# Loading x and the adaLN weights for two blocks of features at a time at the head of a one-core encoder layer

## The chip, the cores and the metric

The kernel runs on one core of one Trainium2 chip. The metric is the device time of one execution in microseconds (us): 1555.84 is the median of three runs (1552.31 to 1558.68). A second number is the profile: one execution recorded by the hardware profiler, whose own time was 1556.39 and whose span, from the first to the last recorded instruction, was 1554.6. Matrix products run on TensorE (PE; its weight loads are PEld), elementwise work on VectorE (DVE), ScalarE (ACT) and GpSimd (POOL); transfers are issued in order by a queue of SyncE (SP) or of POOL and carried out by 16 DMA engines.

## The reference

One layer of a streaming encoder, for a prompt of 1024 tokens and a sample of 32 tokens, width 1024. What matters here is its first step:

```
m = silu(c) @ w_ada + b_ada             # c: one vector per sequence; w_ada: 1024 x 6144
sh1, sc1, g1, sh2, sc2, g2 = split(m, 6)
u = x * (1 + sc1) + sh1                 # 1024 x 1024
z = u @ w_in                            # fq | fk | fv | ff | dq | dk | dv
... forgetting attention, differential attention, output projection,
... layer norm, ConvFFN, layer norm
```

The shift `sh1` and the scale `sc1` of a feature need the whole column of `w_ada` of that feature, and the product `u @ w_in` sums over features, so the kernel can begin the product for a block of features as soon as that block's columns of `w_ada` and its part of `x` are there.

## The kernel before

Features are cut into eight blocks of 128 (k = 0 to 7), tokens into eight blocks of 128. In the first stage, which the change is about, each block k of features goes through these steps:

- **Loads.** `ada_mod` loads 1 MB of `w_ada`: 128 columns for the shift and 128 for the scale, in four transfers of 256 KB (line 175) into tiles of tag `ada` (four buffers, two per block, so two blocks fit). `modulated` loads 512 KB of `x`, 128 features for all tokens (line 317), into a tile of tag `x` (two buffers). For every even k, 512 KB of `w_in` for two blocks come in (`wrfq`, line 320; the "raw" weights).
- **Columns.** 8 products of `silu(c)` with the `w_ada` tiles, column-tiled on PE into the PSUM tile `psAm` (`colmm`; the trace counts two records for each, so 16 for a block). ACT copies them to `asb` (line 181), small products with a selector matrix sum up the groups ("selector products": `psAm<-cst,asb`), and DVE adds the bias and writes `sh`, `sc` (lines 186 and 187).
- **Transposes.** 8 transposes of `x` into two PSUM banks `psx` (line 116), one of tag `pt`, one of tag `ms`. Since `psf` holds the other `pt` bank, the transposes of the next block can write a bank only when ACT and DVE have read it.
- **Modulation.** For each of two halves of 512 tokens, ACT writes the rounded `uh` (line 330), DVE `uf` in full (line 331) and the rest `ul = uf - uh` (line 332).
- **Products.** `products_fq`: for four groups of 128 columns, three matmuls (high with high, low with high, high with low) into `accqa`, `accqb`, for the first 512 tokens only. The raw weights are split into a high and a low part by ACT (line 88) and DVE (line 89) first. For every odd k four products into `psf` (forget gates) follow, which read the `uf` tiles of both blocks.

The order on PE, SP and DVE in this stage is the order of the code (`manual_schedule`); on ACT, on POOL and in the rest of the kernel a scheduler puts the instructions in order from its own estimate of times, so an edit here may also move instructions elsewhere. Semaphores hold each instruction until its inputs are there and its buffer is free. After the stage come, on PE, the one small transpose `psp`, the products of the other 512 tokens (`accqc`, `accqd`), and the five other column groups of `w_in` (`z1` to `z5`).

Around `k`, the body before reads: sums of block k+1, transposes of block k+1, half of the products of block k, modulation of block k+1, columns of block k+2, the other half of the products of block k. Loads are issued two blocks ahead.

Of the kernel before, what the change touches and what calls it, by code (L numbers as in the profile page):

```python
# [8 lines left out]
F32 = mybir.dt.float32  # L9
# [7 lines left out]
P = 128  # L17
# [36 lines left out]
def layer_kernel(ctx: ExitStack, tc: tile.TileContext, a: dict, o: list):  # L54
# [59 lines left out]
    def tr(out, in_):  # L114
        n = in_.shape[0]
        nc.tensor.transpose(out, in_, ident[:n, :n])  # L116
# [52 lines left out]
    def ada_mod(pl, name, kb, j0, sh, sc, tag):  # L169
# [17 lines left out]
        nc.vector.tensor_scalar(sc[:, kb], ps[:, 258:260], b[1], 1.0, ALU.add, ALU.add)  # L187
        yield

    def gate(pl, i, j0, h, tag):  # L190
# [76 lines left out]
    with pool("pa") as pa:  # L267
        def pt_(name, tag, bufs, shape=(P, 1024), dt=F32):
            return pa.tile(list(shape), dt, name=name, tag=tag, bufs=bufs)


        xk0, uf0 = pt_("x0", "x", 2, (P, TT)), pt_("uf0", "x2", 2, (P, TT))
# [38 lines left out]
        nc.gpsimd.dma_start(wff, w_in[:, :, 1536:1544])  # L311
        us_ = {}

        def modulated(k):

            xk = (pt_(f"x{k}", "x", 2, (P, TT)) if k else xk0)[:, 0:T].rearrange("p (b c) -> p b c", b=NB)
            nc.sync.dma_start(xk, xv[:, :, k * P:(k + 1) * P])
            if k % 2 == 0:
                raw = pt_(f"wrfq{k}", "raw", 5, (P, 2, 512)) if k else raw0
                nc.sync.dma_start(raw, w_in[:, k:k + 2, 0:512])  # L320
                raws.append(raw)
            yield
            psx = [b1(f"psx{k}{h}", "ms" if h else "pt") for h in range(2)]
            for i in range(8):
                tr(psx[i // 4][:, i % 4 * P:(i % 4 + 1) * P], xk[:, i])
            yield
            us_[k] = u = (pt_(f"uf{k}", "x2", 2, (P, TT)) if k else uf0)[:, 0:T]
            for h in range(2):
                t = slice(h * 512, (h + 1) * 512)
                nc.scalar.activation(uh[k][:, t], psx[h], AF.Identity, bias=sh1[:, k, 0:1], scale=sc1[:, k, 0:1])  # L330
                nc.vector.tensor_scalar(u[:, t], psx[h], sc1[:, k, 0:1], sh1[:, k, 0:1], ALU.mult, ALU.add)
                nc.vector.tensor_tensor(ul[k][:, t], u[:, t], f(uh[k][:, t]), ALU.subtract)
            yield

        def split_fq(k):
            if k < 5:
                hl = pq.tile([P, 2, 512], F32R, name=f"whfq{k}", tag="qk0", bufs=6)
            else:
                hl = pt_(f"whfq{k}", "hl", 5, (P, 2, 512), F32R) if k > 5 else hl5
            split(hl[:, 0], hl[:, 1], raws[k // 2][:, k % 2])  # L340
            hls.append(hl)

        def products_fq(k, prs, h):
            t = slice(h * 512, (h + 1) * 512)
            for pr in prs:
                c = slice(pr * P, (pr + 1) * P)
                mm3(acc[pr], hls[k][:, 0, c], hls[k][:, 1, c], uh[k][:, t], ul[k][:, t], k == 0, k == KD - 1)

        with tc.manual_schedule(engines={e.engine for e in (nc.tensor, nc.sync, nc.vector)}):
            am = [ada_mod(pa, f"m{k}", k, 0, sh1, sc1, "po") for k in range(KD)]  # L350
            xm = [modulated(k) for k in range(KD)]
            for k in range(2):
                next(am[k])
                next(xm[k])
            next(am[0])
            next(xm[0])
            next(am[0])
            split_fq(0)
            next(xm[0])
            next(am[1])  # L360
            for k in range(KD):
                if k + 2 < KD:
                    next(am[k + 2])
                    next(xm[k + 2])
                elif k + 2 == KD:
                    nc.sync.dma_start(xs[0:TS], a["x_sample"][0])
                    nc.sync.dma_start(rot, a["cst"][:, C_RES:C_END])
                if k + 1 < KD:
                    next(am[k + 1])
                    next(xm[k + 1])  # L370
                    split_fq(k + 1)
                products_fq(k, (0, 1), 0)
                if k % 2 == 1:
                    for j in range(4):
                        kk, h = k - 1 + j % 2, j // 2
                        mm(psf[32 * j:32 * j + 8], wff[:, kk], us_[kk][:, h * 512:(h + 1) * 512], k == 1, k == KD - 1, tile_position=(0, 32 * j))
                if k + 1 < KD:
                    next(xm[k + 1])
                if k + 2 < KD:
                    next(am[k + 2])  # L380
                products_fq(k, (2, 3), 0)
        ps = b1("psp", "ms")
        tr(ps[:, 48:r0 + 17], prow[0:NJ + 17])
        nc.vector.tensor_copy(pcol[:, 48:r0 + 17], ps[:, 48:r0 + 17])
# [18 lines left out]
        ffr = pt_("ffr", "x", 2)[0:8]  # L403
# [62 lines left out]
        def forget():  # L466
            psl = b1("psl", "ms")
            for b in range(NB):
                tr(psl[:, b * 8:(b + 1) * 8], ffr[:, b * P:(b + 1) * P])
            for k in range(KD):  # L470
                colmm(psl[:, 64:72], us[:, k], wff[:, k], k, KD)
            lfp, lfs, lfc = [lg[:, 512 + 64 * i:576 + 64 * i].rearrange("p (b h) -> p b h", h=8) for i in range(3)]
            ffs = lg[0:TS, 704:712]
            sum_groups(ffs, psl[:, 64:72], TS)
            lfs = lfs[0:TS, 0:1]
            nc.sync.dma_start(lfc, a["cache_fox_logf"][0, 0].rearrange("(p j) h -> p j h", j=8))
            log_sigmoid(lfp, psl[:, 0:64].rearrange("p (b h) -> p b h", h=8), P, NB)
# [42 lines left out]

        def ld_a(nm):
            ldn.append(0)
            return pt_(nm, "x" if len(ldn) % 2 else "x2", 2)
# [991 lines left out]
```

## Time and profile before

| | us |
|---|---|
| median of three runs | 1555.84 |
| profiled execution, own time | 1556.39 |
| its span | 1554.6 |
| PE busy | 1482.9 (95%) |
| DVE, ACT, POOL busy | 875.0, 582.1, 422.1 |
| mean granted TensorE clock, share of full | 0.983 |

PE is busy for 95% of the span, so the 71.7 us in which it is not are all that a new order of the same work can win, with what a lower clock costs. The page cuts the span into 40 slices of 38.9 us; in its first slice PE shows a 6, in later ones mostly a 9, and the DMA engines a 9 (this slice is the first stage). Waits of DVE, ACT and POOL cost nothing as long as PE has work.

### The profile page before, as it was taken

What the parts mean: (1) busy time and instruction counts of PE and PEld (TensorE: products, weight loads), DVE (VectorE), ACT (ScalarE), POOL (GpSimd) and SP (SyncE); (2) the same over time, 40 slices, a digit from 0 to 9 for tenths busy, and PEclk for the clock granted to TensorE, in tenths of its full rate; (3) what the DMA queues carried; (4) which work ended last, traced back from release to release, by engine and by line L of the source; (5) the groups of instructions that cost most, each with busy time, mean ns of one, the idle gap of its engine ahead of it and who ended that gap; (6) DMA issues with size and microseconds to landing.
All of it is one profiled execution on the core that took longest, in us unless ns stands there. A gap on an engine that the chain in (4) does not pass through costs nothing.

```text
span 1554.6 us, 23531 instructions
## 1 busy us (share of the span) xinstructions
PE 1482.9 (95%) x8525; PEld 1242.0 (80%) x8525; DVE 875.0 (56%) x1772; ACT 582.1 (37%) x1187; POOL 422.1 (27%) x638
## 2 busy tenths in 40 slices
PE   6999999997989999989999999999999999999996
PEld 4677787765646677777789999999999998888884
DVE  3522217734535799847768886742233236446788
ACT  3311211245646788743654344321121121322332
POOL 0002005734323333323414433455530000000001
PEclk9999999998999999999999999999999999999998
DMA  9623123459775344244448999832231113555863
GB/s 255 190 97 114 55 86 112 122 175 259 189 210 138 96 125 98 85 164 145 150 162 307 337 358 322 295 116 74 80 92 55 41 41 114 183 176 179 288 224 135
DMA packets 221141, 250.52 MB, mean 161 GB/s; under 512 B 14465, under 2 KB 148898, under 8 KB 221026
## 3 DMA queue, kind: packets, MB, share of 16 engines
q1 hardware_dynamic: 210962, 218.65, 45.0%
q0 software_dynamic: 10064, 30.37, 6.6%
q8 instruction: 67, 1.10, 0.3%
q14 instruction: 48, 0.39, 0.1%
HBM read 173.83 MB, written 66.75 MB: 155 GB/s over the span
## 4 chain that ended last, share of the span: by engine, by line
PE 65%; DMA 15%; DVE 9%; issue 4%; SPq 2%; ACT 2%; POOL 2%; POOLq 0%; DVEq 0%; ACTq 0%
PE wd L82 15%; PE up L82 8%; PE upc L82 4%; DMA dwn<-wn 4%; PE wo L82 4%; PE po L82 3%; DMA dres<-rr 3%; DMA rr<-dx 2%; PE Sf L82 2%; PE ptf L116 2%; PE Sd L82 2%; DVE wn L89 2%; PE pod L82 1%; DMA wq<-in_w_down 1%; SPq L175 1%
## 5 line engine op out<-in xcount | busy, mean ns | idle before, releaser
L82 PE MATMUL wd<-ol,oh 128*128 128x512 f32 x308 | 119.4, 390 | 0.0
L82 PE MATMUL wd<-oh,ol 128*128 128x512 f32 x308 | 117.1, 389 | 0.0
L82 PE MATMUL wd<-oh 128*128 128x512 f32 x308 | 112.9, 391 | 2.3 <-DMA oh<-dwn 2.3
L982 POOL TENSOR_TENSOR rstd<-rstd,mhalf 128x1 f32<-128x1 f32 (+1 forms) x18 | 14.5, 814 | 262.3 <-DVE rstd L981 257.6
L1162 POOL TENSOR_TENSOR rr<-rr,gb 128x128 f32<-128x128 f32 (+1 forms) x72 | 45.8, 637 | 117.6 <-DMA rr<-dx 117.2
L629 POOL TENSOR_SCALAR wf<-wf,rs 128x128 f32<-128x128 f32 (+7 forms) x64 | 47.6, 749 | 109.5 <-DVE rs L595 80.1
L82 PEld LDWEIGHTS wd<-oh 128*128 128x128 f32 x308 | 57.6, 188 | 16.6 <-DMA oh<-dwn 2.0
L82 PEld LDWEIGHTS wd<-ol,oh 128*128 128x128 f32 x308 | 57.8, 188 | 12.5 <-DMA ol<-dwn 0.6
L82 PEld LDWEIGHTS wd<-oh,ol 128*128 128x128 f32 x308 | 57.8, 188 | 12.0
L88 ACT CAST oh<-h 128x512 fp32r<-128x512 f32 x44 | 27.2, 621 | 87.3 <-PE wd L82 67.7
L89 DVE TENSOR_TENSOR wh<-wr,wh 128x512 fp32r<-128x512 f32 x40 | 28.7, 742 | 50.9 <-ACT wh L88 50.9
L88 ACT CAST wh<-wr 128x512 fp32r<-128x512 f32 x40 | 24.3, 622 | 85.4 <-DMA wr<-in_w_in 19.0
L594 ACT ACTIVATE wf<-wf,lo 128x128 f32<-128x128 f32 (+7 forms) x64 | 49.5, 776 | 17.8 <-DVE lo L591 15.6
L594 ACT ACTIVATE wd<-wd,lo 128x128 f32<-128x128 f32 (+7 forms) x64 | 49.6, 777 | 13.3 <-DVE lo L591 11.3
L82 PE MATMUL po<-ptpf,vf 128*64 128x256 f32 (+1 forms) x320 | 54.0, 372 | 0.5 <-DVE ptpf L619 0.4
L1205 ACT ACTIVATE cv<-cv 128x1058 f32<-128x1058 f32 x22 | 24.0, 1090 | 76.5 <-DVE cv L1204 76.4
L591 DVE CUSTOM_DVE_ANT_0 wf<-Sf,nb 128x512 f32<-128x512 f32 (+3 forms) x64 | 36.8, 588 | 26.4 <-PE Sf L82 19.1
L1163 POOL TENSOR_TENSOR rr<-rr,gb 128x128 f32<-128x128 f32 (+1 forms) x72 | 50.2, 698 | 5.2
L1200 POOL COPY cvo<-row 128x2 f32<-128x2 f32 x22 | 12.8, 584 | 138.9 <-ACT row L1198 138.9
L89 DVE TENSOR_TENSOR ol<-h,oh 128x512 fp32r<-128x512 f32 x44 | 29.8, 683 | 36.4 <-ACT oh L88 36.4
L1197 ACT COPY row<-up 128x352 f32<-128x352 f32 x44 | 17.7, 455 | 83.4 <-PE up L82 56.8
L116 PE MATMUL ptf<-cst,wf 128*128 128x128 f32 x288 | 47.6, 286 | 1.1 <-POOL wf L629 0.7
(1545 smaller groups left out, 4777.5 us busy)
## 6 DMA issues: line engine op xcount, KB each, us to landing
dwn<-wn SPq DMA_DIRECT2D x154, 256.0 KB
oh<-dwn SPq DMA_DIRECT2D x77, 256.0 KB
ol<-dwn SPq DMA_DIRECT2D x77, 256.0 KB
wq<-in_w_down SPq DMA_DIRECT2D x44, 256.0 KB
wr<-in_w_in SPq DMA_DIRECT2D x20, 512.0 KB
adam<-in_w_ada SPq DMA_DIRECT2D x32, 256.0 KB
adan<-in_w_ada SPq DMA_DIRECT2D x32, 256.0 KB
ga<-in_w_ada SPq DMA_DIRECT2D x16, 512.0 KB
```

Source lines behind the costliest of these rows:

```text
L82: nc.tensor.matmul(out, l, r, start=start, stop=stop, **k)
L88: nc.scalar.copy(hi, src)
L89: (eng or nc.vector).tensor_tensor(lo, src, f(hi), ALU.subtract)
L116: nc.tensor.transpose(out, in_, ident[:n, :n])
L175: nc.sync.dma_start(pga[h][:, :, s, :], w_ada[:, 4 * h:4 * h + 4, c0:c0 + P])
L591: nc.vector.tensor_tensor_reduce(w[:, c], S[:, 0:n], t, -1.0, lo, ALU.add, ALU.min, lo_)
L594: nc.scalar.activation(w[:, 0:ext], w[:, 0:ext], AF.Exp, bias=lo, scale=-1.0, accum_out=sm)
L629: nc.gpsimd.tensor_scalar(w, w, rs, 1.0, ALU.mult, ALU.mult)
L1162: nc.gpsimd.tensor_tensor(r, r, gb[c0][0:n, 0], ALU.mult)
L1163: nc.gpsimd.tensor_tensor(r, r, gb[c0][0:n, 1], ALU.add)
L1197: nc.scalar.copy(row[:, 2 + g * G3:2 + (g + 1) * G3], accs[g])
L1205: nc.scalar.activation(c[:, 0:L], c[:, 0:L], AF.Silu)
```

## The change

The loads of `x` and `w_ada` are made for two blocks at a time: `ada_pair` loads 2 MB in four transfers of 512 KB, with rows of 256 columns (1 KB) in place of 128 columns (512 B), and `load_x` loads 1 MB of `x` for two blocks, also in rows of 1 KB. The memory stays the same: the four `ada` buffers now hold one pair (before, two blocks), and `x` has one buffer of double size (before, two). The columns of a pair are computed in one go, and all 12 products of a block stand in one run.

```diff
+    def ada_pair(pl, name, p, j0, sh, sc, tag):
+        pga = {}
+        for s in range(2):
+            for h in range(2):
+                pga[h, s] = t = pl.tile([P, 4, 2 * P], F32, name=f"ada{name}{h}{s}", tag="ada", bufs=4)
+                c0 = (j0 + s) * D + 2 * p * P
+                nc.sync.dma_start(t, w_ada[:, 4 * h:4 * h + 4, c0:c0 + 2 * P])
+        yield
...
+                colmm(ps[:, s * 256:(s + 1) * 256], cT[:, k, :], pga[k // 4, s][:, k % 4], k, KD)
+            asb.append(ca.tile([P, 256], F32, name=f"asb{s}", tag="s256", bufs=4))
+            nc.scalar.copy(asb[s], ps[:, s * 256:(s + 1) * 256])
+        yield
...
+        def load_x(p):
+            t = xk0 if p == 0 else pt_(f"x{p}", "x", 1, (P, 2 * TT))
+            xp_[p] = t = t[:, 0:2 * T].rearrange("p (b c) -> p b c", b=NB)
+            nc.sync.dma_start(t, xv[:, :, 2 * p * P:2 * (p + 1) * P])
...
-            for k in range(2):
-                next(am[k])
-                next(xm[k])
             next(am[0])
+            load_x(0)
+            load_raw(0)
             next(xm[0])
+            next(am[0])
             next(am[0])
             split_fq(0)
             next(xm[0])
-            next(am[1])
             for k in range(KD):
...
+                p = k // 2
+                if k % 2 == 0 and p + 1 < KD // 2:
+                    next(am[p + 1])
+                    load_raw(p + 1)
                 if k + 1 < KD:
-                    next(am[k + 1])
                     next(xm[k + 1])
+                if k % 2 == 0:
+                    if p + 1 < KD // 2:
+                        load_x(p + 1)
...
+                products_fq(k, range(4), 0)
+                if k + 1 < KD:
                     split_fq(k + 1)
-                products_fq(k, (0, 1), 0)
-                if k % 2 == 1:
+                if k % 2 == 0:
+                    next(xm[k + 1])
+                    if p + 1 < KD // 2:
+                        next(am[p + 1])
+                else:
+                    if p + 1 < KD // 2:
+                        next(am[p + 1])
+                        next(xm[k + 1])
...
-                if k + 1 < KD:
-                    next(xm[k + 1])
-                if k + 2 < KD:
-                    next(am[k + 2])
-                products_fq(k, (2, 3), 0)
...
-                lft = pt_(f"lft{s}", "x", 2, (P, TT))[0:8]
+                lc = pt_(f"lc{s}", "x", 1, (P, 2 * TT))[0:8]
+                lft = lc[:, 0:TT]
...
-                cum = pt_(f"cum{s}", "x", 2, (P, TT))[0:8]
+                cum = lc[:, TT:2 * TT]
```

On SP, at the start of the program, the loads stand as follows before; `adam` are tiles of `w_ada`, `x` and `wrfq` those of `x` and of the raw weights:

```order
L175 DMA adam_153<-in_w_ada 128x4x128 x2
L175 DMA adam_154<-in_w_ada 128x4x128 x2
L317 DMA x_108<-in_x_prompt 128x8x128
L320 DMA wrfq_110<-in_w_in 128x2x512
L175 DMA adam_161<-in_w_ada 128x4x128 x2
L175 DMA adam_162<-in_w_ada 128x4x128 x2
L317 DMA x_167<-in_x_prompt 128x8x128
```

In the changed program the same place of SP reads, with the semaphores that each instruction waits for (`PE` stands for products that must have read the buffer, `DMAHW` for an earlier transfer):

```order
L197 DMA adam_159<-in_w_ada 128x4x256
L347 DMA x_108<-in_x_prompt 128x8x256 [waits DMAHW0_49]
L351 DMA wrfq_110<-in_w_in 128x2x512 [waits DMAHW1_49]
L485 DMA bfb<-in_b_f 128x8 [waits DMAHW2_49]
L545 DMA t_129<-in_conv_w 66x128 [waits DMAHW3_49,PE_49]
L546 DMA t_129<-in_state_ffn_conv 44x128 [waits DMAHW4_49]
L547 DMA t_129<-in_lambda_vecs 128x256 [waits DMAHW5_49]
L197 DMA adam_211<-in_w_ada 128x4x256 [waits DMAHW6_49,PE_49]
L197 DMA adam_213<-in_w_ada 128x4x256 [waits DMAHW7_49,PE_49]
L197 DMA adam_215<-in_w_ada 128x4x256 [waits DMAHW0_49,PE_49]
L197 DMA adam_217<-in_w_ada 128x4x256 [waits DMAHW1_49,PE_49]
L351 DMA wrfq_219<-in_w_in 128x2x512 [waits DMAHW2_49]
```

The `x` of the first blocks now stands behind 2 MB of `w_ada` in place of 1 MB, and the second pair of `w_ada` waits for products of the first.

On PE, between the products of block 1 and those of block 2, the program before reads (`psAm_313<-cst,asb` are the selector products of block 2, `psx_344`, `psx_345` the transposes of block 3):

```order
L82 MATMUL psAm_313<-adam_271,cT 32x256 x4
L82 MATMUL psAm_313<-adam_272,cT 32x256 x4
L82 MATMUL accqb<-uh_113,whfq_238 128x512
L82 MATMUL accqb<-ul_121,whfq_238 128x512
L82 MATMUL accqb<-uh_113,whfq_238 128x512 x2
L82 MATMUL accqb<-ul_121,whfq_238 128x512
L82 MATMUL accqb<-uh_113,whfq_238 128x512
L82 MATMUL psAm_313<-cst,asb 128x2 x2
L116 MATMUL psx_344<-cst,x_277 128x128 x4
L116 MATMUL psx_345<-cst,x_277 128x128 x4
L82 MATMUL accqa<-uh_114,whfq_293 128x512
```

Between the same products, the changed program reads (`asb_264`, `asb_274` belong to blocks 2 and 3, `psx_330`, `psx_331` are the transposes of block 3, `uh_114` is block 2):

```order
L82 MATMUL accqb<-uh_113,whfq_245 128x512
L82 MATMUL psAm_255<-cst,asb_264 128x2 x2
L82 MATMUL psAm_255<-cst,asb_274 128x2 x2
L82 MATMUL psf<-uf_109,wff 8x512
L82 MATMUL psf<-uf_248,wff 8x512
L82 MATMUL psf<-uf_109,wff 8x512
L82 MATMUL psf<-uf_248,wff 8x512
L116 MATMUL psx_330<-cst,x_231 128x128 x4
L116 MATMUL psx_331<-cst,x_231 128x128 x4
L82 MATMUL accqa<-uh_114,whfq_298 128x512
```

Before, the transposes of block 2 stood ahead of block 1's products, and half of those products stood behind the start of block 2's columns; now nothing but `psf` stands between the selector products of a pair and the transposes that need the banks of its modulation. In the attention stage, which the diff does not touch, the scheduler has put many pieces of PE's program in another order too.

## Rows read from the trace of the kernel before

**Rows 1.** Busy time by stretch: engine busy us, granted clock, DMA share, GB/s.
```profile
0.00:67.00 67.00, 50.85 (x333) 34.53 (x334) 32.72 (x70) 23.45 (x39) 3.78 (x10) 0.95 0.92 243
67.00:135.00 68.00, 68.00 (x316) 53.48 (x315) 14.41 (x24) 10.29 (x16) 4.37 (x6) 1.00 0.21 71
```
**Rows 2.** Stretches with 512 B rows alone, and with 2 and 4 KB rows.
```profile
40.00:44.00 4.00, 4.00 (x34) 3.08 (x27) 2.62 (x6) 2.34 (x5) 0.00 (x0) 1.00 1.19 291
100.00:103.00 3.00, 3.00 (x15) 2.48 (x14) 0.59 (x2) 0.75 (x2) 0.54 (x1) 1.00 1.02 387
```
**Rows 3.** Order of time on PE: start, us, engine, line, what, count [idle before].
```profile
12.37 1.97 PE L116 MATMUL psx<-cst,x 128*128 128x128 f32 x8 [0.60 <-DMA x<-in_x_prompt]
...
17.36 1.08 PE L82 MATMUL psAm<-adam,cT 128*32 128x256 f32 x8 [0.64 <-DMA adam<-in_w_ada]
...
21.39 0.78 PE L82 MATMUL accqa<-uh,whfq 128*128 128x512 f32 x1
...
28.93 0.61 PE L82 MATMUL psAm<-cst,asb 128*128 128x2 f32 x4 [2.67 <-ACT asb L181]
...
55.62 0.61 PE L82 MATMUL psAm<-cst,asb 128*128 128x2 f32 x4 [2.10 <-ACT asb L181]
```
**Rows 4.** The chain of work that ended last: start, us, what.
```profile
25.96 1.14 ACT whfq L88 x2
...
31.16 2.31 PE accqa L82 x6
33.47 0.97 PE psf L82 x8
...
37.24 0.93 PE psx L116 x8
38.17 1.39 PE accqa L82 x6
39.56 1.00 PE psAm L82 x16
...
42.16 0.36 PE psAm L82 x4
...
72.82 0.18 PE psp L116
```
**Rows 5.** The two stretches with a lower granted clock.
```profile
30.00:35.00 5.00, 5.00 (x36) 3.25 (x34) 1.02 (x2) 1.55 (x2) 0.00 (x0) 0.70 1.06 273
55.00:60.00 5.00, 4.38 (x22) 3.21 (x26) 2.56 (x6) 2.02 (x4) 0.00 (x0) 0.69 1.06 252
```
**Rows 6.** Order of time on DVE, one block's modulation.
```profile
37.47 0.21 DVE L186 TENSOR_SCALAR sh<-psAm,pcol 128x2 f32<-128x2 f32 x1
...
38.72 0.81 DVE L331 TENSOR_SCALAR uf<-psx,sc,sh 128x512 f32<-128x512 f32 x1 [0.31 <-ACT uh L330]
...
40.17 0.80 DVE L331 TENSOR_SCALAR uf<-psx,sc,sh 128x512 f32<-128x512 f32 x1
...
42.63 0.22 DVE L186 TENSOR_SCALAR sh<-psAm,pcol 128x2 f32<-128x2 f32 x1 [0.92 <-PE psAm L82]
```
**Rows 7.** Order of time on ACT: the same modulation; a cast waiting for its load; the scan's copy.
```profile
37.91 1.45 ACT L330 ACTIVATE uh<-psx,sh,sc 128x512 fp32r<-128x512 f32 x2 [2.16 <-DVE sc L187]
...
102.25 1.14 ACT L88 CAST wh<-wr 128x512 fp32r<-128x512 f32 x2 [2.62 <-DMA wr<-in_w_in]
...
166.70 1.19 ACT L492 COPY lft<-pslt 8x512 f32<-8x512 f32 x1 [4.89 <-PE pslt L116]
```
**Rows 8.** Order of time on SP: that load with three more; the scan's result.
```profile
96.88 2.50 SPq L534 DMA_DIRECT2D wr<-in_w_in  x4
...
164.15 0.30 SPq L503 DMA_DIRECT2D dcump<-cum  x1
```
**Rows 9.** PE's waits, 310 to 660 us: us in total, times, longest.
```profile
PE psAn L82 <- DMA adan<-in_w_ada: 7.3, 3, 4.6
PE psG L82 <- DMA ga<-in_w_ada: 3.6, 1, 3.6
```

More of the change, by code (lines that the diff above doesn't have):

```diff
@@ L188, in ada_mod @@
         yield
+    def ada_pair(pl, name, p, j0, sh, sc, tag):
[6 more added lines that the diff above has]
+        yield
+        ps = b1(f"psA{name}", tag)
+        asb = []
+        for s in range(2):
+            for k in range(KD):
+                colmm(ps[:, s * 256:(s + 1) * 256], cT[:, k, :], pga[k // 4, s][:, k % 4], k, KD)
+            asb.append(ca.tile([P, 256], F32, name=f"asb{s}", tag="s256", bufs=4))
+            nc.scalar.copy(asb[s], ps[:, s * 256:(s + 1) * 256])
+        yield
+        for s in range(2):
+            for q in range(2):
+                i = 4 * s + 2 * q
+                mm(ps[:, i:i + 2], asb[s][:, q * P:(q + 1) * P], cst[:, C_SEL2:C_SEL2 + 2], True, True)
+        for q in range(2):
+            kb = 2 * p + q
+            b = [bcol[:, (j0 + s) * 8 + kb:(j0 + s) * 8 + kb + 1] for s in range(2)]
+            nc.vector.tensor_scalar(sh[:, kb], ps[:, 2 * q:2 * q + 2], b[0], None, ALU.add)
+            nc.vector.tensor_scalar(sc[:, kb], ps[:, 4 + 2 * q:6 + 2 * q], b[1], 1.0, ALU.add, ALU.add)
+        yield
     def gate(pl, i, j0, h, tag):
@@ L269, in pt_ @@
             return pa.tile(list(shape), dt, name=name, tag=tag, bufs=bufs)
-        xk0, uf0 = pt_("x0", "x", 2, (P, TT)), pt_("uf0", "x2", 2, (P, TT))
+        xk0, uf0 = pt_("x0", "x", 1, (P, 2 * TT)), pt_("uf0", "x2", 2, (P, TT))
         raw0 = pt_("wrfq0", "raw", 5, (P, 2, 512))
@@ L312, in layer_kernel, with load_raw @@
         us_ = {}
-        def modulated(k):
[L316 to L322, printed above, removed]
+        xp_ = {}
+        def load_x(p):
+            t = xk0 if p == 0 else pt_(f"x{p}", "x", 1, (P, 2 * TT))
+            xp_[p] = t = t[:, 0:2 * T].rearrange("p (b c) -> p b c", b=NB)
+            nc.sync.dma_start(t, xv[:, :, 2 * p * P:2 * (p + 1) * P])
+        def load_raw(p):
+            raw = pt_(f"wrfq{p}", "raw", 5, (P, 2, 512)) if p else raw0
+            nc.sync.dma_start(raw, w_in[:, 2 * p:2 * p + 2, 0:512])
+            raws.append(raw)
+        def modulated(k):
             psx = [b1(f"psx{k}{h}", "ms" if h else "pt") for h in range(2)]
             for i in range(8):
-                tr(psx[i // 4][:, i % 4 * P:(i % 4 + 1) * P], xk[:, i])
+                tr(psx[i // 4][:, i % 4 * P:(i % 4 + 1) * P], xp_[k // 2][:, i, k % 2 * P:(k % 2 + 1) * P])
             yield
@@ L349, in layer_kernel @@
         with tc.manual_schedule(engines={e.engine for e in (nc.tensor, nc.sync, nc.vector)}):
-            am = [ada_mod(pa, f"m{k}", k, 0, sh1, sc1, "po") for k in range(KD)]
+            am = [ada_pair(pa, f"m{p}", p, 0, sh1, sc1, "po") for p in range(KD // 2)]
             xm = [modulated(k) for k in range(KD)]
-            for k in range(2):
-                next(am[k])
-                next(xm[k])
             next(am[0])
+            load_x(0)
+            load_raw(0)
             next(xm[0])
+            next(am[0])
             next(am[0])
@@ L359, in layer_kernel @@
             next(xm[0])
-            next(am[1])
             for k in range(KD):
-                if k + 2 < KD:
-                    next(am[k + 2])
[L364 to L367, printed above, removed]
+                p = k // 2
+                if k % 2 == 0 and p + 1 < KD // 2:
+                    next(am[p + 1])
+                    load_raw(p + 1)
                 if k + 1 < KD:
-                    next(am[k + 1])
                     next(xm[k + 1])
-                    split_fq(k + 1)
-                products_fq(k, (0, 1), 0)
-                if k % 2 == 1:
+                if k % 2 == 0:
+                    if p + 1 < KD // 2:
+                        load_x(p + 1)
+                    else:
+                        nc.sync.dma_start(xs[0:TS], a["x_sample"][0])
+                        nc.sync.dma_start(rot, a["cst"][:, C_RES:C_END])
+                products_fq(k, range(4), 0)
+                if k + 1 < KD:
+                    split_fq(k + 1)
+                if k % 2 == 0:
+                    next(xm[k + 1])
+                    if p + 1 < KD // 2:
+                        next(am[p + 1])
+                else:
+                    if p + 1 < KD // 2:
+                        next(am[p + 1])
+                        next(xm[k + 1])
                     for j in range(4):
@@ L376, in layer_kernel @@
                         mm(psf[32 * j:32 * j + 8], wff[:, kk], us_[kk][:, h * 512:(h + 1) * 512], k == 1, k == KD - 1, tile_position=(0, 32 * j))
-                if k + 1 < KD:
-                    next(xm[k + 1])
-                if k + 2 < KD:
-                    next(am[k + 2])
-                products_fq(k, (2, 3), 0)
         ps = b1("psp", "ms")
@@ L402, in layer_kernel @@
         nc.vector.tensor_tensor(us, us, sh1[:, :, 1:2].to_broadcast([P, KD, TS]), ALU.add)
-        ffr = pt_("ffr", "x", 2)[0:8]
+        ffr = pt_("ffr", "x", 1, (P, 2 * TT))[0:8]
         for h in range(2):
@@ L522, in ld_a @@
             ldn.append(0)
-            return pt_(nm, "x" if len(ldn) % 2 else "x2", 2)
+            return pt_(nm, "x", 1, (P, 2 * TT))[:, 0:T] if len(ldn) % 2 else pt_(nm, "x2", 2)
         for i, c0, op, os_ in ((1, 512, p_fk, s_fk), (2, 1024, p_fv, s_fv), (4, 2056, p_dk, s_dk), (3, 1544, None, None), (5, 2568, p_dv, s_dv)):
```

## The prediction

> **What bounds the kernel now.** I read first the busy time by stretch, then the order of time on PE, then the chain of work that ended last, and the granted clock last. From 67 to 135 us PE has no idle time at all [rows 1]: what the first stage ends late or early there goes to the end of the span, as the product of the other 512 tokens and the next column groups need nothing but PE. The point to watch is the start of `psp`, 72.8 us [rows 4]. Up to 67 us PE is busy for 50.9 only, and the DMA engines for 92% of the stretch [rows 1]. The first 21.4 us pass before the first product [rows 3]; what is late there is each time a load of `w_ada` or `x` (idle 0.60 and 0.64 in front of PE, ended by DMA). After that PE idles twice, 2.67 us before 28.93 and 2.10 before 55.62, both times for a copy `asb` on ACT [rows 3], which stood behind a cast of raw weights whose load came late (the chain passes through that cast at 25.96 [rows 4]). After both the granted clock is lower, 0.70 and 0.69 over 5 us [rows 5], which costs 5 × 0.30 and 5 × 0.31, some 3 us. So the stage is bound by the loads at its head and nearly balanced between loads and PE behind it.
>
> How much work PE has for two blocks at the full clock: transposes 2 × 0.93, products 4 × 1.39, columns 2 × 1.00, selector products 2 × 0.36 and `psf` 0.97 [rows 4], together 11.1 us. The loads for two blocks are 2 MB + 1 MB + 0.5 MB = 3.67 million bytes, at 291 GB/s [rows 2] 12.6 us. That is why it is the loads now.
>
> **The change part by part.**
>
> *Wider rows.* `w_ada` and `x` come in rows of 1 KB. No row here shows that size. In rows of 512 B the engines moved 291 GB/s, in a stretch with 2 and 4 KB rows 387 [rows 2]; these are the ends. Taken as a fixed part and a part by the byte, with 2 KB for the latter (16 × 512 / 291 = 28.2 ns a packet, 16 × 2048 / 387 = 84.7), 1 KB needs 47 ns, or 348 GB/s. I take that estimate. A pair's `w_ada` then takes 6.0 us, its `x` 3.0. The loads of two blocks fall to 10.5 us, under PE's 11.1, so bandwidth is no longer the bound, and its gain is worth only what PE can use of it.
>
> The Trainium skill (DMA: Bandwidth & Descriptors, Specifications) puts the smallest transfer that reaches line rate at 512 B, by which 1 KB would gain nothing. The two rates of rows 2 speak against it. By the rule the head below would be 1.8 us longer and two transfers of `x` 0.6 each, in all 3.0 us more than my sum.
>
> *The head.* Before, the transposes of block 0 could start at 12.37, behind 1 MB of `w_ada` and 0.5 MB of `x`; at 17.36 PE went on with the last tile of block 1's `w_ada`, when 3.1 million bytes of these loads had been issued up to it [rows 3]. Now `x` stands behind 2 MB of `w_ada` and is 1 MB itself, the same 3.15 million bytes. At the old rate block 0 starts at 17.4; at 348 GB/s these bytes take 9.0 in place of 10.8 us, so 15.6 (15 to 17.4). PE's order now puts the transposes ahead of the columns, so the columns, whose data has been there for a while, wait for `x`. Transposes 1.97 and columns of two blocks 4 × 1.08, at the low clock that both show at this place [rows 3], end at 21.9; I take 21.5, as the clock may rise under them. Copy and selector products take 1.0: 22.5. Then the modulation of block 0 has to free the banks before the transposes of block 1, and only behind these stand the products.
>
> *The wait for the banks.* From the end of the selector products (42.16 + 0.36) to `sh` it takes 0.11 [rows 4, 6]; from `sh` to `uh` 0.44, from `uh` to `uf` 0.81, and `uf` takes 0.81 [rows 6, 7]; two more small DVE operations for the second block add 0.3. So the first bank is free after 2.5 us, the second (40.17 + 0.80 − 37.91 = 3.06 behind `uh`) after 3.9, and with half of the transposes behind it the products can start 4.4 us after the selector products. Before, half of a block's products and the next columns lay beside this; now PE has `psf`, 0.97, and the transposes, 0.93: 2.5 us of idle time for each pair.
>
> Block 0's products thus start at 26.9, not at 21.4. They begin at the low clock (the first six took 2.31 in place of 1.39 after the idle time at 28.9 [rows 4]); for twelve I take 2.78 + 1.3 = 4.1, end 31.0. Columns of the next pair 2.0, transposes of block 2 0.93, products of block 1 2.78, selector products 0.72: 37.4. The load of that `x`, issued at 26.9 behind the second pair's `w_ada` (free from 18.7 on, done about 27) and raw weights, is there at about 32.8, in time for 33.0.
>
> *The single buffers.* The next `x` can be issued only when the transposes of the odd block have read the tile, 4.4 us behind the selector products, with a queue that has run empty by then. PE wants it after 2.78 of products and 2.00 of columns, 4.8 us later. The nearest row: four loads issued from 96.88 on, the first of them usable at 102.25, 5.4 us for 512 KB, of which 1.4 is transfer at 387 GB/s, beside other traffic [rows 2, 7, 8]. With 3.0 us of transfer in place of 1.4 this makes 7.0; the transfer alone makes 3.0. I take 6.0, nearer to the row, so 1.2 us of idle time per pair (0 to 2.2). `w_ada` of the next pair is released by the columns and wanted some 13 us later; its 6.0 and the raw weights' 1.4 lie beside PE's work.
>
> *The sum.* From one pair's selector products to the next: 4.4 + 2.78 + 2.00 + 1.2 + 0.93 + 2.78 + 0.72 = 14.8 us. Twice that from 37.4 is 67.0. Then 4.4, two blocks of products 5.56 and `psf` 0.97: 77.9. Some of the idle time at three places (2.5 and 1.2 close together) will lower the clock as the two of before did (1.5 each [rows 5]); I take one of three (0 to 4.5): 79.4. Against 72.8 this is 6.6 us later.
>
> *Edits at nothing.* The number of products, transposes, casts and copies is the same. Casts of raw weights now stand on ACT ahead of a half of `uh` (blocks 1, 3, 5); the half behind them frees the second bank only, which is wanted some 5 us later; if their load is late, that is what queues there. The scan of the forget gates now shares one buffer, so the copy for the sample waits until the result of the prompt is stored: issued at 164.15, copied again at 166.70 [rows 7, 8], 2.5 us that cover one small store; uncovered it would cost about 1 us.
>
> The profiled execution took 1556.39, of which the span is 1554.6; 6.6 more is 1563.0. The median of three is 0.55 lower, so I say 1562.4.
>
> **The rivals.**
>
> *The gaps close (not slower).* If the banks came back sooner (the second transposes waiting for ACT alone, as the first reader), or the low clock of before, 3 us, and its two waits, 4.8 us, went without new ones, a pair would take PE's 11.1 and little more. The deciding point: (72.8 − 37.4 − 10.9) / 2 = 12.2 us for a pair; below it the change wins. At 11.6 `psp` starts at 71.5, time 1554. For it: loads below PE's work. Against it: the order on PE, in which no product stands between.
>
> *It waits more (slower still).* 1 KB rows stay at 291 GB/s (head 17.4, `x` 3.6) and the clock falls at all three places: 1.8 + 1.2 + 3.0 more than the forecast, 1568.4. For it: in the rows both idle times of over 2 us were followed by it. Against it: `psf` and transposes lie between the new ones.
>
> *The attention stage decides.* The scheduler moved PE's work and some loads there too. PE waits 7.3 us for `adan` and 3.6 us for `ga` [rows 9]; these could go or grow by half: 1551.5 to 1568. Nothing in the profile says which.
>
> That the change doesn't do what it says is out: the order shows the new loads and places.
>
> **How the numbers follow.** Forecast (`psp` 3 to 10 us later, 1559 to 1566) 0.60, gaps close 0.14, waits more 0.14, attention 0.12, half of it each way. A measurement here tells 0.5%, 7.8 us, from no change. Slower than 1563.6: a third of the forecast (0.21), the third case, half of the fourth: 0.41. Faster than 1548: little of the second and the fourth, 0.07. The rest, 0.52, is within. The forecast's own range is 1559 to 1566; the range for 8 in 10 runs from 1553, for the gaps that close, to 1570.
>
> **What would show it.** Right: the first product at about 27, `x` of block 0 at about 15.6, idle time before `psx` ended by DVE `uf` and by DMA `x` at each pair, transfers that pause, `psp` near 79. Wrong: `x` not before 19 or before 14, PE without idle time after the selector products, DMA still at 90% to 60 us, or the first stage as forecast and a change of several us behind 310.

## The result and the profile after

The changed kernel takes 1563.87 us, median of 11 runs, against 1555.84 of before on the same chip: 1.0055 of the time, with a 95% interval of 1.0039 to 1.0071. So it is 8.0 us slower; the forecast was 1562.4. The profiled execution took 1562.35, its span is 1560.6, 6.0 more than before. `psp` starts at 81.67 us (forecast 79.4), 8.9 later than before.

The busy time by stretch, with the columns and the stretches of [rows 1]; the last three lines are the parts of the first stage with a low granted clock (the column before the DMA share):

```profile
0.00:67.00 67.00, 42.45 (x285) 28.56 (x286) 26.88 (x58) 20.12 (x35) 3.46 (x10) 0.90 0.75 242
67.00:135.00 68.00, 67.23 (x325) 52.48 (x323) 19.97 (x35) 13.29 (x20) 4.67 (x7) 1.00 0.21 71
26.00:32.00 6.00, 5.03 (x15) 4.15 (x16) 4.63 (x8) 1.81 (x3) 0.00 (x0) 0.52 0.72 243
42.00:47.00 5.00, 4.58 (x18) 3.73 (x19) 4.04 (x6) 2.49 (x4) 0.00 (x0) 0.66 0.32 106
57.00:63.00 6.00, 4.92 (x18) 3.94 (x19) 5.13 (x9) 3.52 (x6) 0.00 (x0) 0.72 0.63 222
```

PE is busy for 42.45 us up to 67 where it was 50.85, and the DMA engines have become less busy too (0.75 in place of 0.92): over the stretch as a whole neither bounds it (in the head PE does wait for a load, until 15.44). PE's order of time, as in [rows 3], with the head, the first pair and `psp`:

```profile
15.44 1.97 PE L116 MATMUL psx<-cst,x 128*128 128x128 f32 x8 [10.84 <-DMA x<-in_x_prompt]
17.34 1.93 PE L82 MATMUL psAm<-adam,cT 128*32 128x256 f32 x16
19.85 1.85 PE L82 MATMUL psAm<-adam,cT 128*32 128x256 f32 x16 [0.58 <-ACT asb L205]
22.21 1.05 PE L82 MATMUL psAm<-cst,asb 128*128 128x2 f32 x8 [0.50 <-ACT asb L205]
...
26.97 1.09 PE L116 MATMUL psx<-cst,x 128*128 128x128 f32 x4 [3.22 <-DVE uf L364]
27.71 0.78 PE L82 MATMUL accqa<-uh,whfq 128*128 128x512 f32 x1
...
32.51 1.07 PE L82 MATMUL psAm<-adam,cT 128*32 128x256 f32 x16
34.07 1.07 PE L82 MATMUL psAm<-adam,cT 128*32 128x256 f32 x16 [0.49 <-ACT asb L205]
35.08 1.09 PE L116 MATMUL psx<-cst,x 128*128 128x128 f32 x8
...
39.67 1.04 PE L82 MATMUL psf<-uf,wff 128*8 128x512 f32 x8
41.97 1.12 PE L116 MATMUL psx<-cst,x 128*128 128x128 f32 x4 [1.25 <-DVE uf L364]
43.50 1.09 PE L116 MATMUL psx<-cst,x 128*128 128x128 f32 x4 [0.42 <-DVE uf L364]
44.24 0.78 PE L82 MATMUL accqa<-uh,whfq 128*128 128x512 f32 x1
...
47.69 1.07 PE L82 MATMUL psAm<-adam,cT 128*32 128x256 f32 x16
49.30 1.07 PE L82 MATMUL psAm<-adam,cT 128*32 128x256 f32 x16 [0.55 <-ACT asb L205]
50.30 1.10 PE L116 MATMUL psx<-cst,x 128*128 128x128 f32 x8
...
81.67 0.25 PE L116 MATMUL psp<-cst,t 39*128 39x39 f32 x1
```

Read from the top: `x` ends the wait at 15.44; columns and selector products follow; the second half of block 1's transposes waits 3.22 for `uf`; block 0's products start at 27.71 and take until 32.51, 4.8 us for 2.78 of work at the full clock. From the end of the selector products (39.67, where `psf` starts) to the next products it is 4.57 us, with two waits for `uf`. The transposes at 35.08 and 50.30 do not wait for `x` at all.

### The profile page after: what moved, and what is told of

It reads as the page before. It is cut to its first block, busy times and chain, and to the rows that moved or that the text cites. A ratio compares the mean times of both kernels' runs of the same rounds, so it can differ in the third digit from the quotient of the medians.

```text
span 1560.6 us, 23485 instructions
## 1 busy us (share of the span) xinstructions
PE 1480.3 (95%) x8525; PEld 1240.9 (80%) x8525; DVE 871.5 (56%) x1772; ACT 581.6 (37%) x1187; POOL 417.9 (27%) x638
## 4 chain that ended last, share of the span: by engine, by line
PE 65%; DMA 15%; DVE 11%; issue 4%; ACT 2%; POOL 2%; SPq 2%; POOLq 0%; DVEq 0%; ACTq 0%
PE wd L82 14%; PE up L82 8%; DMA dwn<-wn 4%; PE upc L82 4%; PE wo L82 4%; PE po L82 3%; DMA dres<-rr 3%; DMA rr<-dx 2%; PE Sf L82 2%; PE ptf L116 2%; PE Sd L82 2%; PE pod L82 2%; DVE wn L89 2%; DMA wq<-in_w_down 1%; PE accqa L82 1%
## 5 line engine op out<-in xcount | busy, mean ns | idle before, releaser
L633 ACT ACTIVATE wf<-wf,lo 128x128 f32<-128x128 f32 (+7 forms) x64 | 49.5, 775 | 18.6 <-DVE lo L630 15.9
L82 PE MATMUL po<-ptpf,vf 128*64 128x256 f32 (+1 forms) x320 | 50.4, 369 | 0.5 <-ACT ptpf L655 0.5
L1239 POOL COPY cvo<-row 128x2 f32<-128x2 f32 x22 | 12.4, 562 | 139.9 <-ACT row L1237 139.9
L630 DVE CUSTOM_DVE_ANT_0 wf<-Sf,nb 128x512 f32<-128x512 f32 (+3 forms) x64 | 36.8, 588 | 23.1 <-PE Sf L82 14.8
L88 ACT CAST wn<-wt 128x512 fp32r<-128x512 f32 x33 | 20.5, 622 | 74.0 <-issue 27.1
```

What stands on the lines that cost most here:

```text
L88: nc.scalar.copy(hi, src)
L630: nc.vector.tensor_tensor_reduce(w[:, c], S[:, 0:n], t, -1.0, lo, ALU.add, ALU.min, lo_)
L633: nc.scalar.activation(w[:, 0:ext], w[:, 0:ext], AF.Exp, bias=lo, scale=-1.0, accum_out=sm)
```

## The experiments

Each was timed against the kernel before, which had a median of 1556.26 in the first four (29 runs) and 1557.60 in the others (35 runs).

| | `psp` starts | span | median | of before, 95% |
|---|---|---|---|---|
| before | 72.75 | 1554.6 | | |
| changed | 81.67 | 1560.6 | 1563.87 | 1.0055 [1.0039, 1.0071] |
| e1_head | 74.26 | 1555.8 | 1558.42 | 1.0026 [1.0005, 1.0046] |
| e2_order | 77.50 | 1560.5 | 1559.12 | 1.0028 [1.0010, 1.0047] |
| e3_both | 69.25 | 1550.9 | 1552.27 | 0.9971 [0.9952, 0.9989] |
| e4_rows512 | 81.10 | 1566.3 | 1565.40 | 1.0069 [1.0041, 1.0096] |
| e5_narrow | 82.89 | 1563.3 | 1567.61 | 1.0062 [1.0043, 1.0081] |
| e6_copies | 77.04 | 1558.1 | 1565.15 | 1.0049 [1.0028, 1.0069] |
| e7_half | 71.67 | 1549.7 | 1553.25 | 0.9976 [0.9956, 0.9996] |
| e8_all | 70.78 | 1558.4 | 1560.16 | 1.0016 [0.9996, 1.0036] |

**The columns first.** Edit, in the head:

```diff
             load_raw(0)
-            next(xm[0])
             next(am[0])
             next(am[0])
+            next(xm[0])
```

> The changed kernel, with the columns and selector products of the first pair put ahead of the transposes of block 0; all else as it is. In the changed kernel the columns stand behind transposes that wait for x until 15.44 us, and the first product starts at 27.71. Theory A (order on PE makes the loss; of its 8.9 us in the first stage about 6 are the head): columns run while x still loads; selector products, sh and sc are then done about 5 us earlier. The copies asb may still queue on ACT behind casts of raw weights that land at 16.9, so I expect a gain of 2.5 to 4 us: first product at 24 to 25, psp at 78 to 79 (81.67 now), time 3 us less, about 1561. Rival B (the bytes bound the head: block 0 cannot start before x is there, whatever stands ahead of it): first product within 1 us of 27.7, psp within 1 us of 81.7, time the same. Rival C (the first stage isn't what decides, PE's reordered attention stage is): psp may move, the time does not.

PE's order of time, then ACT's, in this kernel:

```profile
13.81 1.87 PE L82 MATMUL psAm<-cst,asb 128*128 128x2 f32 x8 [0.49 <-ACT asb L205]
15.54 2.80 PE L116 MATMUL psx<-cst,x 128*128 128x128 f32 x12
21.09 1.12 PE L116 MATMUL psx<-cst,x 128*128 128x128 f32 x4 [2.75 <-DVE uf L364]
21.86 0.78 PE L82 MATMUL accqa<-uh,whfq 128*128 128x512 f32 x1
```
```profile
13.38 0.37 ACT L205 COPY asb<-psAm 128x256 f32<-128x256 f32 x1 [3.24 <-PE psAm L82]
16.78 1.14 ACT L88 CAST whfq<-wrfq 128x512 fp32r<-128x512 f32 x2 [3.02 <-DMA wrfq<-in_w_in]
17.83 2.10 ACT L363 ACTIVATE uh<-psx,sh,sc 128x512 fp32r<-128x512 f32 x3
```

The first product comes at 21.86 in place of 27.71, and `psp` 7.4 us earlier, twice what was expected: the copies at 9.77 and 13.38 are over before the casts, which I had feared ahead of them, can start. The transposes of block 0 start at 15.54, 0.1 later than in the changed kernel and straight behind the selector products, so they gain nothing. So theory A holds, its size was too small, and B is out: 5.85 us of what stood behind the transposes had no need to. The other 1.5 us came by the clock: block 0's products took 4.1 us in place of 4.8, and block 2's ran at the full clock behind waits of 1.26 and 0.88, where those of the changed kernel began at the low one.

**Modulation ahead of the odd block's products.** Edit (the same lines leave their old places behind `products_fq`):

```diff
+                if k % 2 == 1:
+                    for j in range(4):
+                        kk, h = k - 1 + j % 2, j // 2
+                        mm(psf[32 * j:32 * j + 8], wff[:, kk], us_[kk][:, h * 512:(h + 1) * 512], k == 1, k == KD - 1, tile_position=(0, 32 * j))
+                    if k + 1 < KD:
+                        split_fq(k + 1)
+                        next(am[p + 1])
+                        next(xm[k + 1])
                 products_fq(k, range(4), 0)
```

> The changed kernel, with one edit in the loop: behind the products of an even block, the four psf products, the casts, the selector products and the modulation of the next block stand ahead of the 12 products of the odd block, so that these lie beside the modulation that frees the banks. Theory A (between selector products and the next first product PE idles 2.65 us three times, 4.55 less psf and transposes, because nothing covers the wait for the banks, and this idle time lowers the clock, which costs about 3 us more): the three waits for uf go, 8 us, and 0 to 3 us of clock; x could be late by 0 to 1 us for each pair; psp at 71 to 75 in place of 81.67; first product unchanged at 27.7; time 7 to 10 us less, 1554 to 1557. Rival B (loads bound the stage): idle time only changes its name, from uf to x or adam, psp stays above 79, time within 2 us of 1563.9. Rival C (the attention stage decides): psp falls as in A, the time does not.

PE's order of time behind the selector products of the first pair:

```profile
42.19 0.60 PE L116 MATMUL psx<-cst,x 128*128 128x128 f32 x4
43.24 0.63 PE L116 MATMUL psx<-cst,x 128*128 128x128 f32 x4 [0.46 <-DVE uf L364]
...
48.79 1.07 PE L82 MATMUL psAm<-adam,cT 128*32 128x256 f32 x16 [1.17 <-ACT asb L205]
```

The direction is A's, the size is half: `psp` 4.2 us earlier, expected 7 to 10. A part of the shortfall lies in the head, which the edit does not touch: the first product came at 28.48 (27.71 in the changed kernel) and block 0's products ended at 33.86 (32.51), most of them at 0.63 us a product, the low clock. Behind block 0 the gain is 5.5 us. The waits for `uf` of the changed kernel in the stretches concerned are 1.25, 0.42, 1.25, 0.88 and 0.77, together 4.6, of which two of about 0.46 are left. My 8 us came from 3 × (4.55 less the shortest durations of `psf` and transposes); in the changed kernel transposes in the gap took longer at the low clock, and the third time a column group of the next stage already stood in it. The wait for `asb` grows from 0.55 to 1.17 in one pair, as the copy now meets the modulation on ACT.

**Both.** The two edits together.

> Both edits: the columns of the first pair ahead of the transposes of block 0, and the psf, selector products and modulation ahead of the odd block's products. Theory A: the gains add, psp at 67 to 71 (before the change 72.75, with it 81.67), time 1550 to 1555, faster than both kernels by 1 to 5 us. Rival B (loads bound the stage): once PE's order stops waiting, x or w_ada is late instead, and psp doesn't fall below 74. Rival C (the attention stage decides): psp falls but the time stays within 2 us of 1563.9.

Busy time by stretch, then two transposes and `psp` from PE's order of time:

```profile
0.00:67.00 67.00, 52.27 (x351) 34.75 (x352) 33.40 (x71) 23.83 (x40) 4.39 (x11) 1.00 0.77 243
67.00:135.00 68.00, 68.00 (x313) 54.40 (x312) 14.32 (x24) 10.91 (x17) 4.55 (x7) 1.00 0.21 71
```
```profile
41.12 1.07 PE L116 MATMUL psx<-cst,x 128*128 128x128 f32 x8 [0.18 <-DMA x<-in_x_prompt]
...
54.45 1.06 PE L116 MATMUL psx<-cst,x 128*128 128x128 f32 x8 [0.54 <-DMA x<-in_x_prompt]
...
69.25 0.25 PE L116 MATMUL psp<-cst,t 39*128 39x39 f32 x1
```

`psp` starts at 69.25, 12.4 us earlier than in the changed kernel (7.4 + 4.2 = 11.6: they add), with a granted clock of 1.00 up to 67 in place of 0.90. The time is below both kernels: 1552.27, 0.9971 of before (0.9952 to 0.9989). What was lost lay in the order on PE: another order wins it back with the same loads in pairs. Whether the wider loads themselves win or lose against single ones is not shown, since no run has this order with the loads of before. Now `x` is late, 0.18 and 0.54.

**The width of the rows.** Each load of `w_ada` and `x` becomes two of 512 B rows:

```diff
-                nc.sync.dma_start(t, w_ada[:, 4 * h:4 * h + 4, c0:c0 + 2 * P])
+                for q in range(2):
+                    nc.sync.dma_start(t[:, :, q * P:(q + 1) * P], w_ada[:, 4 * h:4 * h + 4, c0 + q * P:c0 + (q + 1) * P])
...
-            nc.sync.dma_start(t, xv[:, :, 2 * p * P:2 * (p + 1) * P])
+            for q in range(2):
+                nc.sync.dma_start(t[:, :, q * P:(q + 1) * P], xv[:, :, (2 * p + q) * P:(2 * p + q + 1) * P])
```

> The changed kernel, but each of its loads of w_ada and x with rows of 1 KB issued as two loads with rows of 512 B (the same bytes, buffers and order of work; four more issues on SP per pair for w_ada, one for x). It isolates what the width of the rows is worth. Theory A (a 1 KB row is carried at 348 GB/s in place of 291, and the order on PE, not bandwidth, makes the loss): the transposes of block 0 start about 1.8 us later, 17.2 in place of 15.44, and x may be late by about 0.6 twice: psp 2 to 3 us later, 83.5 to 84.7, time 1566. Rival B (the width is worth nothing, line rate is reached at 512 B): start of block 0 within 0.5 us of 15.44, psp within 0.7 of 81.67, time the same. Rival C (the wide rows themselves cost time, by spreading a load over fewer packets): psp earlier, time less.

Block 0 started at 15.94, `psp` came at 81.10: by the numbers B. But the run did not measure what it was made for: with two loads block 0 needs only the first, 0.5 MB less. So it was run again with the odd block's load first:

```diff
-            for q in range(2):
+            for q in (1, 0):
                 nc.sync.dma_start(t[:, :, q * P:(q + 1) * P], xv[:, :, (2 * p + q) * P:(2 * p + q + 1) * P])
```

> As the run with 512 B rows before it, but of the two loads that make up x for two blocks the one for the odd block is issued first. In that run block 0 needed only the first of the two loads, 0.5 MB less than in the changed kernel, so its start (15.94 us) did not measure the width alone. Here block 0's transposes wait for the load issued last, as many bytes as in the changed kernel. Theory A (width counts: from 5 to 14 us the changed kernel moved some 335 GB/s, the run with 512 B rows some 255): block 0 starts at 17.2 to 18, first product at 29 to 30, psp at 82.5 to 84. Rival B (the width is worth nothing): block 0 starts at 15.4 to 16.2, psp at 81 to 82.

PE's order of time, and the stretch 5 to 14 us (GB/s last) in the changed kernel and here:

```profile
17.41 1.97 PE L116 MATMUL psx<-cst,x 128*128 128x128 f32 x8 [12.86 <-DMA x<-in_x_prompt]
...
50.90 1.06 PE L116 MATMUL psx<-cst,x 128*128 128x128 f32 x8 [0.38 <-DMA x<-in_x_prompt]
```
```profile
5.00:14.00 9.00, 0.00 (x0) 0.00 (x0) 0.00 (x0) 0.00 (x0) 0.00 (x0) 1.00 1.09 335
```
```profile
5.00:14.00 9.00, 0.00 (x0) 0.00 (x0) 0.00 (x0) 0.00 (x0) 0.00 (x0) 1.00 1.07 261
```

Theory A: with the same bytes ahead of it block 0 starts 2.0 us later, and `x` is late by 0.38 and 0.57 in the pairs. The run also has twice as many loads, and SP has issued both halves of `x` by 12.2 us, where the one load of `x` was issued by 6.0. In both runs the DMA engines are as busy (1.07 and 1.09), which speaks for the rows and against a queue that ran empty, but no run separates the width from the number of loads. `psp` moves by 1.2 only; part came back where products ran at a higher clock (from 42 to 47 us 1.00, in the changed kernel 0.66). In time the width can't be told apart here (1.0062 and 1.0055, with intervals that overlap).

**The copies.** The changed kernel's waits of 0.58, 0.49, 0.55 and 0.55 for `asb`:

```diff
+        for s in range(2):
             asb.append(ca.tile([P, 256], F32, name=f"asb{s}", tag="s256", bufs=4))
             nc.scalar.copy(asb[s], ps[:, s * 256:(s + 1) * 256])
```

> The changed kernel, with the two copies asb of a pair both behind the columns of its second half, in place of one copy behind each half. In the changed kernel the second half's columns wait for the copy of the first half, which reads the same PSUM tile: 0.58, 0.49, 0.55 and 0.55 us. Theory A (that wait is a cost of its own): the four waits go, psp 1.7 to 2.3 us earlier than 81.67, at 79.4 to 80, time 1562. Rival B (it is given back, since the later copy now holds up the selector sums, the first of them above all): psp within 0.6 us of 81.67.

Two issues of `x` on SP, and the transposes that wait for them on PE:

```profile
26.55 0.37 SPq L348 DMA_DIRECT2D x<-in_x_prompt  x1
42.10 0.37 SPq L348 DMA_DIRECT2D x<-in_x_prompt  x1
```
```profile
33.01 1.09 PE L116 MATMUL psx<-cst,x 128*128 128x128 f32 x8 [0.52 <-DMA x<-in_x_prompt]
...
47.22 1.06 PE L116 MATMUL psx<-cst,x 128*128 128x128 f32 x8 [0.53 <-DMA x<-in_x_prompt]
```

`psp` comes 4.6 us earlier, more than the waits and more than theory A's 1.7 to 2.3: in the stretches 42 to 47 and 57 to 63 the granted clock is 1.00 here, where it was 0.66 and 0.72. In exchange `x` is late. But the time is not lower (1565.15; expected 1562), and the runs reach from 1556.72 to 1573.53 with mean clocks from 0.986 to 0.976. A second trace was taken for that, beside one of each kernel:

> The version with the copies asb behind both halves, unchanged, for a second trace. Its first trace had psp 4.6 us earlier than the changed kernel, but its median was no lower, and its runs were spread over 17 us at granted clocks of 0.976 to 0.986 (the traced run had 0.986). Theory A (the order gains the 4.6 us in the first stage in every run; what is lost is lost later, by a lower clock): psp at 76.5 to 77.5 again, and a span over 1561 with a stretch of low clock behind 300 us. Rival B (the first trace was lucky in the first stage: its products ran at the full clock): psp at 79 or later in this trace.

`psp` at 77.41, span 1557.3: the gain in the first stage repeats, but this run was not a long one either, and shows no loss behind 300 us. Where the longer runs lose it stays open.

**Block 0's products sooner.** On top of e3_both, the first six products of block 0 ahead of block 1's transposes:

```diff
+                if k == 0:
+                    products_fq(0, (0, 1), 0)
                 if k + 1 < KD:
                     next(xm[k + 1])
```

> The version with both edits (psp 69.25 there), with one more: the first six products of block 0 stand ahead of the transposes of block 1, so that they lie beside the wait for the banks that is left in the head (2.60 us, for uf). Theory A (that idle time is the same wait for banks as in the pairs): the first product starts at 19 to 20.3 in place of 21.34 and the wait is gone or under 0.6 us; psp at 67 to 68.2; time 1 to 2 us less than the 1552.27 of that version. Rival B (the products wait for ul, which comes no sooner than the banks; and x of the next pair, issued behind the transposes, comes late): psp within 0.6 of 69.25, time the same.

PE's order of time, the head and two later transposes:

```profile
19.02 0.80 PE L82 MATMUL accqa<-uh,whfq 128*128 128x512 f32 x1 [1.17 <-ACT uh L363]
20.73 0.80 PE L82 MATMUL accqa<-ul,whfq 128*128 128x512 f32 x1 [0.92 <-DVE ul L365]
...
30.17 1.09 PE L116 MATMUL psx<-cst,x 128*128 128x128 f32 x8 [0.82 <-DMA x<-in_x_prompt]
...
56.90 1.06 PE L116 MATMUL psx<-cst,x 128*128 128x128 f32 x8 [0.92 <-DMA x<-in_x_prompt]
```

The first product does start at 19.02, and the wait for the banks is gone, but `psp` comes 2.4 us later than in e3_both. That is rival B's mechanism, though B had `psp` unchanged within 0.6: the products wait for `ul`; the odd block's transposes, and with them the issue of the next `x`, come later (24.97 for 21.71), and PE waits for that `x`. The time is that of e3_both.

**All edits together.** e7_half with the copies moved as in e6_copies.

> All edits together: columns of the first pair first, modulation ahead of the odd block's products, six products of block 0 ahead of block 1's transposes, copies asb behind both halves of the columns. Theory A: the gains add, psp at 65 to 67, time 1548 to 1550.5, some 6 us faster than the kernel before the change and some 14 faster than the changed one. Rival B (loads bound what is left): waits for x or w_ada grow by what the others lose, psp at 68 to 69.

`x` is late by 1.53, 0.46 and 1.97, `psp` starts at 70.78, outside both forecasts, and the time, 1560.16, is no better than before. The waits are rival B's: the load of `x` into its single buffer is what is left in the stage, though no run with a second buffer was made. By the ratios it is some 7 us over e3_both (1.0016 and 0.9971), far more than the 1.5 us of `psp`. The two traces show where these two executions part: e8_all is 1.5 us behind at `psp`, 3.1 at the first `wo2x` product with `wow01h`, which before has at 685.54, and 7.5 at the first `upc` product with `wu141h` (1138.30 in before). The two traces of before are 4.2 us apart at the first of these products too, so why, here as with the copies alone, stays open.

**A second trace of both kernels.**

> The changed kernel unchanged, for a second trace. In its first trace the span was 1560.6, 6.0 over that of before, though psp was 8.9 late and stayed so until 1128 us; there every other trace so far has a wait of 2.4 to 2.9 us for the cast wu141h, and that trace has none. Theory A (the wait is left out by luck of that run; the change costs what its first stage costs): psp within 0.5 us of 81.67, the wait for wu141h back, span near 1563. Rival B (the change takes that wait away for good): no wait there, span near 1560.6.

> The kernel before, unchanged, for a second trace. Theory A (the first stage repeats to a few tenths, later stages differ by a few us from run to run): psp within 0.5 of 72.75, wait for wu141h of 2 to 3 us, span 1551 to 1559. Rival B (the first stage itself varies by several us, so that the 8.9 us between two single traces say little): psp off by over 1.5 us.

`psp` repeats: 81.11 and 72.55. The spans are 1559.3 and 1555.1. But theory A on `wu141h` (the high part of a block of `w_up`, cast on ACT) falls. PE's waits from 1100 to 1150 us (total, times, longest), in the second trace of the changed kernel and in the first of before:

```profile
PE up L82 <- DVE wu141l L89: 0.7, 1, 0.7
PE up L82 <- ACT wu141h L88: 0.5, 1, 0.5
```
```profile
PE up L82 <- ACT wu141h L88: 2.6, 1, 2.6
PE up L82 <- DVE wu141l L89: 0.4, 1, 0.4
```

It is no luck of one run. SP issues that weight's load here, in before and in the changed kernel:

```profile
1123.49 0.39 SPq L869 DMA_DIRECT2D wu141r<-in_w_up  x1
```
```profile
1128.63 0.39 SPq L908 DMA_DIRECT2D wu141r<-in_w_up  x1
```

The issue is 5.1 us later, the end of PE's work in front of it (`upc` with `wu140l`) 8.75. With the wait gone PE is some 3 us nearer to before behind that place, in both traces of the changed kernel. But it is not that a PE which comes later waits less. In e5_narrow PE's work in front ends 8.6 us later than in before, as in the changed kernel; there SP issues the load 8.7 us later, at 1132.19, and the wait is back, as it is in e4_rows512 (10.7, 10.5 and a wait of 2.42):

```profile
1137.09 0.43 PE L82 MATMUL up<-u2h,wu141h 128*128 128x352 f32 x1 [2.50 <-ACT wu141h L88]
```

So what counts is when SP issues that load against PE's pace; why it is early in the changed kernel alone stays open.

## Why the prediction was right

The forecast of 1562.4, by a first stage that ends later because of its order, was 1.5 us off, inside its own range of 1559 to 1566; 8.0 us lies just beyond the bound of 7.8 that it drew between the same and slower. The path was right: the head, then the wait for the banks at each pair, and PE without a reserve behind them. That the number is so near is in part luck: an `x` wait that did not come (2 × 1.2) stood against low clock and a wait for `asb` that were too small or missing, so that `psp` came only 2.3 us later than forecast, and some 3 us were given back at `wu141h`, far behind the stage, of which the forecast knew nothing. Its steps:

- *Wider rows and the head.* 15.6 forecast, 15.44 measured; at the old rate 17.4 forecast, and 17.41 measured in e5_narrow, an agreement that is partly chance: e5_narrow moved 261 GB/s there, not the 291 that the forecast took. The Trainium skill (DMA: Bandwidth & Descriptors, Specifications) has line rate from 512 B on, by which the width would be worth nothing. The traces disagree, with 335 against 261 GB/s and those 2.0 us, and the measurement decides; the number of loads, named at e5_narrow, stays as a rival of the width. First product: 26.9 forecast, 27.71 measured.
- *The wait for the banks.* 4.4 us from selector products to products forecast, 4.57 measured; e2_order shows that it comes from the order: with products in the gaps the waits for `uf` there fall from 4.6 to 0.9, and `psp` comes 4.2 us earlier although the head of that run was 1.4 later.
- *The single buffer.* This step failed: 1.2 us of idle time for `x` in each pair, and in the changed kernel there is none. From issue to use `x` takes what I took (6.0): 5.1 and 6.5 in e6_copies. What was wrong is the time until PE wants it, 4.8 us: slow columns, waits for `asb` and products at a low clock make it 7.0 (28.09 to 35.08) and 5.7 (44.62 to 50.30). With some of these gone the wait appears, in e3_both, e6_copies, e7_half and e8_all.
- *The low clock.* 1.3 us in block 0 and 1.5 at one other place forecast; measured 2.0 (4.8 less 2.78), 0.7 in block 2 (44.24 to 47.69) and 1.65 in block 4, 4.35 in place of 2.8. Mis-sized by 1.5 us.
- *Not foreseen:* the columns' second half waits for the copy of the first; both halves lie in one tile, which fills one PSUM bank. This costs some 0.5 us three times in the pairs, and e6_copies takes it away. By a rule of the Trainium skill (PSUM — Partial Sum Buffer, PSUM bank collisions raise a hardware error) a wait has to be there: semaphores are to keep accesses apart by bank, or by bank and group of 32 partitions, not by address. The idle rows 0.49 to 0.58 agree with it as the price; no run here shows what the two halves would do without the wait.
- *The sum.* 79.4 forecast, 81.67 measured. At the end of block 1's selector products it is 2.3 late (37.4, 39.67): 0.8 at the first product, 0.7 in block 0's products, 0.5 for `asb` and the rest in small pieces. The two pairs took 15.2 and 15.9 in place of 14.8 (1.5 more, in which clock and `asb` outweigh the missing 2 × 1.2). The last part was right (10.9), and the 1.5 of low clock that the forecast had added at the end is already in the pairs, so that `psp` is late by the 2.3 of the head alone.
- *Edits at nothing, and all that follows.* PE's shift against before stays near 8.93 from `psp` to past 300 us (8.92 at the first `z5d` product, 310.01 in before), so the scan's shared buffer cost nothing.

*The rivals.* The gaps did not close by themselves (15.2 and 15.9 for a pair, deciding point 12.2), but in e3_both, with 13.3 (41.12 to 54.45), they did nearly, and the head gave the rest: this case needs another order. "It waits more" was half right, in the clock. "The attention stage decides" is out for the kernel as a whole: within that stage PE's order differs, so that the transposes `pkcf`, at 499.26 us in before, start at 499.11, with no shift at all; but the `wo` products behind the stage, 685 us in before, start 8.7 later again. The second trace of the changed kernel does the same (8.4 at `psp`, −0.3 and 7.0). Before's own second trace is 4.2 us off its first at 685, so single traces can't settle 4 us there.

## What to carry to other kernels

When loads are made wider, write the order of the consumers anew from what arrives first: in the head the first product came 5.85 us earlier once work whose loads stood ahead of `x` was no longer behind its transposes. What stands between the last reader of a bank and its next writer decides the wait; put independent products there, and count the clock that the idle time costs. After each gap that is closed, look for the next wait: here the load of `x` into its single buffer, which had been hidden by the others.

## What the runs showed of the hardware

A gap of 1 to 3 us on PE was followed by products at a granted clock of 0.52 to 0.72 in some cases and not in others: with the same waits of 1.25 and 0.88 for `uf`, the products behind ran at 1.00 in e6_copies, and in the changed kernel's stretch 57 to 63 at 0.72. In e1_head both happen in one execution: behind such waits a product took 0.39 us from 37.67 on, and 0.63 from 52.21 on. And between 20 and 23 us the first products of e3_both took 0.63 us (full clock: 0.39) while the granted clock stands at 1.00:

```profile
20.00:23.00 3.00, 2.43 (x8) 2.14 (x9) 3.00 (x7) 1.70 (x3) 0.00 (x0) 1.00 1.09 362
```
```profile
21.34 0.78 PE L82 MATMUL accqa<-uh,whfq 128*128 128x512 f32 x1
21.91 0.63 PE L82 MATMUL accqa<-ul,whfq 128*128 128x512 f32 x1
```
